# A hybrid decoder step on one core: prompt attention and paged decode rewritten as 16 steps in the order of the text

## The chip, the cores and the metric

One Trainium2 chip, of which the kernel uses one core. The metric is the device time of one execution in microseconds, given as the median of several runs. TensorE (PE in the profile, with PEld for its weight loads) does the matrix products and the transposes, VectorE (DVE) and ScalarE (ACT) the elementwise work and the copies out of PSUM, GpSimd (POOL) little, and SyncE (SP) issues the transfers.

## The reference, cut to what matters

One layer of a hybrid decoder, for a prompt of 1024 tokens and for 8 sample tokens (one each) that stand behind 4096 cached positions. The model width is 1024, all in float32.

```python
def hybrid_layer(x, pos, lw, gla_mix, mla_attend):
    x = x + 0.5 * swiglu(rms_norm(x, f1n), f1g, f1u, f1d)
    h = rms_norm(x, mix_n)
    q, k, v, g, a_low, c_q, c_kv, k_pe_raw = jnp.split(h @ w_in, offsets, axis=-1)
    o_gla, S = gla_mix(*gla_inputs(q, k, v, a_low, w_a_up, b_a))
    y_gla = gla_output(o_gla, g, g_norm)
    q_nope, q_pe, lat, k_pe = mla_project(c_q, c_kv, k_pe_raw, pos, q_norm, kv_norm, w_uq)
    y_mla = mla_attend(q_nope, q_pe, lat, k_pe, w_uk, w_uv)
    x = x + jnp.concatenate([y_gla, y_mla], axis=-1) @ w_out
    x = x + 0.5 * swiglu(rms_norm(x, f2n), f2g, f2u, f2d)
    return x, lat, k_pe, S
```

The change lies in `mla_attend`. For the prompt, each of 4 heads makes keys (`lat @ w_uk`) and values (`lat @ w_uv`) from a latent of 128 numbers per token, rotates 64 of the query's numbers by position, and takes a causal softmax over 1024 positions. For the samples the latents of the past are gathered by a page table (32 pages of 128 positions for each of 8 samples), the queries are taken into the latent's space (`q_lat = q_nope @ w_uk`), and the softmax runs over 4097 positions.

## The kernel before, in words

Products that must keep float32 accuracy are made of three (`mm3`, L87): each operand is split into a high part in the fast format and a rest (`split`, L83: ScalarE copies the high part, VectorE subtracts it), and high times high, high times low and low times high are summed in one PSUM bank. The stages follow each other: first feed-forward (0 to 717 us), input projection (to 850), the linear attention (GLA, to some 1021), prompt attention with paged decode (to 1314), output projection (to 1411), second feed-forward (to 2099).

A generator `pages` copies cache pages into gathered buffers in DRAM (`kvd`, `ped`); `beside(n)` (L199) takes its next n copies, which SyncE issues at that place. It is called in each block of `seven` (L295) in the first feed-forward, in the input projection (L761), and once for all that is left ahead of `levels(0, ..)` (L1051).

The paged decode has 16 units, `dec_unit(g, u)` (L1191): 2 groups of 4 samples by 8 stretches of 512 positions. A unit loads four tiles `kvt` and four `pet` (six buffers each), turns them on TensorE (16 transposes of `kvt`, 8 of `pet`, four to a bank, which ScalarE copies to `latT` and VectorE to `peT`), makes the scores (`dsc`), takes VectorE's maximum (`stat`) and ScalarE's exponential (`dpp`), turns that (VectorE copies it to `dpT`), multiplies it with `kvt` and keeps the result in `oc`. All its PSUM tiles rotate through the two banks of `psD`. `dec_combine(g)` joins a group's units and the new token.

Two units are run beside the end of GLA. Then the prompt's heads follow: for each pair of heads the rotary queries (`qpr`, `qs`) and all eight value tiles, for each head both key tiles, and for each block m of 256 queries `scores(m)` (L1366), the turns and products of the block before (`outputs`, L1414), and one decode unit. `scores` makes the queries, the products for two tiles of 128 queries (`sc`, three banks), the row maximum, the exponentials into one tile `pp` of 1024 columns, and scales it by the reciprocal of the sum. `outputs` turns `pp` in groups of four into `pT_h` and `pT_l` (three buffers each) and multiplies them with the values into `po` (one bank), whose split is `ym_h`, `ym_l`. Queries, keys, values and the turns of `pp` share the two banks `psA_`.

The order of the work on each engine is set when the kernel is built: a scheduler that keeps the tiles' dependencies orders instructions by their priority, which falls in the order of the text, and it may move one ahead of another. At run time each engine takes its instructions in that order.

Of the kernel before, what the change touches and what calls it, by code (L numbers as in the profile page):

```python
# [67 lines left out]
def hybrid_step(ctx: ExitStack, tc: tile.TileContext, I, O, C):  # L68
# [226 lines left out]
    def seven(A, todo):  # L295
# [3 lines left out]
        for i in (1, 6, 2, 7, 5, 3, 4):  # L299
# [18 lines left out]
            beside()  # L318
# [438 lines left out]
    def win_tile(src, evict, wt=None, blocks=BLKS3):  # L757
        if wt is None:
            wt = win_weights(src)
        h, l, n = wt  # L760
        beside(2)  # L761
# [74 lines left out]
    def rope(pool_, tag, dst, src, n, s):  # L836

        L = s.stop - s.start
        W = 512 if tag == "pp" else BL
        w = pool_.tile([P, 2 * W], F32, name="ropew", tag=tag, bufs=3 if tag == "pp" else 1)  # L840
# [101 lines left out]
    def levels(qr, st):  # L942
# [6 lines left out]
        for li, sz in enumerate((64, 32, 16, 8, 4, 2, 1)):  # L949
            qt = qts[nq[0] % 2]  # L950
            nq[0] += 1
            E = gk.tile([P, 2, 256], F32, name="E", tag="E")
# [98 lines left out]
    beside(len(units) * 16)  # L1051
# [99 lines left out]

    early_raw = []
    for srcs in ([qnd[:, 0]], [qnd[:, 1]], [latd], [kpd, kpd]):
        raw = rawp.tile([P, SEQ], F32, name="raw", tag="raw")
        w = P // len(srcs)
        for i, src in enumerate(srcs):
            ld.dma_start(raw[i * w:(i + 1) * w], src)
# [4 lines left out]
    psD_cm, psd = pool("psD", 2, space=PSUM, side="right")  # L1162

    def dbank(name="pd"):
        return psd.tile([P, 512], F32, name=name, tag="pd")
# [6 lines left out]
    oT = ep.tile([P, NS, 32], F32, name="oT", bufs=1)  # L1172
    uv = ep.tile([P, 4, P], F32, name="uv", bufs=1)
    ld.dma_start(uv, w_uv)
    grp = {}

    def fetch(g, u):

        kvt = [ep.tile([P, J, P], F32, name="kvt", tag="kvt", bufs=6) for _ in range(4)]
        pet = [ep.tile([P, J, 64], F32, name="pet", tag="pet", bufs=6) for _ in range(4)]  # L1180
# [3 lines left out]
        return kvt, pet  # L1184
# [6 lines left out]
    def dec_unit(g, u):  # L1191

        if u == 0:
            grp[g] = (ep.tile([P, 3, NU + 1], F32, name="stat", tag="stat"), ep.tile([P, NU + 1, P], F32, name="oc", tag="oc", bufs=1))
        oc = grp[g][1]
        kvt, pet = fetch(g, u)
        sc = dbank("dsc")
        lt, pe = [], []
        for b2 in range(2):
            p = dbank()  # L1200
            for q in range(4):
                PE.transpose(p[:, q * P:(q + 1) * P],
                             pet[2 * b2 + q // 2][:, 2 * (q % 2):2 * (q % 2) + 2, :].rearrange("p j c -> p (j c)"), ident)
            peT = ep.tile([P, 512], F32, name="peT", tag="peT")
            V.tensor_copy(peT, p)
            pe += [peT[:, :256], peT[:, 256:]]
        for bi in range(4):
            p = dbank()
            for q in range(4):
                PE.transpose(p[:, q * P:(q + 1) * P], kvt[bi][:, 2 * (q % 2) + q // 2, :], ident)  # L1210
            lt.append(ep.tile([P, 512], F32, name="latT", tag="latT", bufs=4))
            S.activation(lt[bi], p, AF.Copy)
        rows = [slice(32 * bi, 32 * bi + 32) for bi in range(4)]
        for bi in range(4):
            PE.matmul(sc[rows[bi], :], qlp[:, 4 * g + bi], lt[bi], start=True, stop=False)  # L1215
        for par in range(2):
            for bi in range(4):
                PE.matmul(sc[rows[bi], par * 256:par * 256 + 256], qpp[par][:, 4 * g + bi], pe[bi], start=False, stop=par == 1)  # L1218
        pp = ep.tile([P, 512], F32, name="dpp", tag="dpp")
        softmax(g, u, sc, 512, pp)  # L1220
        pT = ep.tile([P, J, P], F32, name="dpT", tag="dpT")
        p = dbank()
        for q in range(4):
            PE.transpose(p[:, q * P:(q + 1) * P], pp[:, q * P:(q + 1) * P], ident)
        V.tensor_copy(pT.rearrange("p j q -> p (j q)"), p)
        po = dbank()
# [3 lines left out]
        V.tensor_copy(oc[:, u], po[:, :P])  # L1230

    def dec_combine(g):
        stat, oc = grp[g]

        p = dbank()
        for bi in range(4):
            b = 4 * g + bi
            PE.matmul(p[32 * bi:32 * bi + 32, :NS], qlp[:, b], lat_s, start=True, stop=False)
            PE.matmul(p[32 * bi:32 * bi + 32, :NS], qpp[0][:64, b], kp_s, start=False, stop=True)
        sn = ep.tile([P, NS], F32, name="sn", tag="sn")  # L1240
        V.tensor_add(sn, p[:, :NS], newmask[:, g * NS:(g + 1) * NS])
        pn = ep.tile([P, NS], F32, name="pn", tag="pn")
        softmax(g, NU, sn, NS, pn)
        p = dbank()
        PE.transpose(p[:NS, :P], pn, ident)
        pnT = ep.tile([NS, P], F32, name="pnT", tag="pnT", bufs=1)
        V.tensor_copy(pnT, p[:NS, :P])
        p = dbank()
# [3 lines left out]
        cm = ep.tile([P, 4], F32, name="cm", tag="cm")  # L1252
        V.tensor_reduce(cm[:, 0:1], stat[:, 0, :], AX.X, OP.min)
        S.activation(stat[:, 2, :], stat[:, 0, :], AF.Exp, bias=cm[:, 0:1], scale=-1.0)
        V.tensor_mul(stat[:, 1, :], stat[:, 1, :], stat[:, 2, :])
        V.tensor_reduce(cm[:, 2:3], stat[:, 1, :], AX.X, OP.add)
        V.reciprocal(cm[:, 3:4], cm[:, 2:3])
        om = ep.tile([P, P], F32, name="om", tag="om", bufs=1)
        V.tensor_scalar_mul(om, oc[:, 0], stat[:, 2, 0:1])
        for u in range(1, NU + 1):  # L1260
            V.scalar_tensor_tensor(om, oc[:, u], stat[:, 2, u:u + 1], om, op0=OP.mult, op1=OP.add)
        V.tensor_scalar_mul(om, om, cm[:, 3:4])
        p = dbank()
# [428 lines left out]
```

## Time and profile before

| what | value |
|---|---|
| median of 3 runs | 2098.72 us (2098.38 to 2100.55) |
| the profiled execution | 2100.9 us |
| its span | 2099.1 us |
| its mean granted clock of TensorE | 0.989 |
| TensorE, VectorE, ScalarE busy | 2031.5, 1471.5, 838.0 us |

The span goes from the first to the last recorded instruction, and 1.8 us of the execution's time lie around it. The profiled execution is 2.2 us over the median of the runs. In the rows below, "PEclk" is the granted clock as a share of full speed, "idle before" is the time in which the engine did nothing ahead of an instruction, and "<-" names what ended it.

### The profile page before, as it was taken

To read this page: it belongs to the slowest core of one execution; us is meant where nothing else is said; L and a number is where in the kernel's file an instruction comes from. 1 tells how busy PE (TensorE), PEld (TensorE's weight loads), DVE (VectorE), ACT (ScalarE), POOL (GpSimd) and SP (SyncE) were. 2 spreads that over 40 slices of the span, in tenths; PEclk is the share of its full clock that TensorE was granted. 3 is DMA by queue.
4 is the path that set the end of the run, shared out by engine and by line. 5 is a ranking of instruction groups with operands and counts; after the bars stand their busy time and mean duration, and the time that the engine had idled before them with its cause. 6 is when DMAs were issued, how large, how long until landed. Compare 5 with 4: busy or idle time off the path is not lost.

```text
span 2099.1 us, 42793 instructions
## 1 busy us (share of the span) xinstructions
PE 2031.5 (97%) x16379; PEld 1915.6 (91%) x16379; DVE 1471.5 (70%) x2902; ACT 838.0 (40%) x1563; POOL 64.1 (3%) x95
## 2 busy tenths in 40 slices
PE   9999999999999999889899999999999999999997
PEld 8999999999999988888667777799999999999997
DVE  7876676675777865766565766488777778766775
ACT  7432322233344530436554644244323323333534
POOL 0000000000000000311000000000000000000000
PEclk9999999999999999999999999999999999999999
DMA  6444445467565623012443342744323233574352
GB/s 215 130 144 141 127 126 152 131 203 265 159 187 152 166 75 99 11 42 81 129 129 96 115 128 60 221 136 122 91 92 121 87 88 122 159 260 146 110 158 92
DMA packets 235837, 276.46 MB, mean 132 GB/s; under 512 B 27216, under 2 KB 186128, under 8 KB 235632
## 3 DMA queue, kind: packets, MB, share of 16 engines
q1 hardware_dynamic: 235632, 273.72, 42.7%
q8 instruction: 129, 2.11, 0.4%
q14 instruction: 76, 0.62, 0.1%
HBM read 214.34 MB, written 84.47 MB: 142 GB/s over the span
## 4 chain that ended last, share of the span: by engine, by line
PE 80%; DVE 8%; DMA 3%; ACT 3%; issue 2%; SPq 1%; POOL 1%; POOLq 0%; DVEq 0%; ACTq 0%
PE pp L93 34%; PE pp L448 20%; PE pw L93 6%; PE pr L93 4%; PE po L93 1%; PE pd L1210 1%; PE pw L1076 1%; PE dsc L1215 1%; DVE al L85 1%; PE pg L973 1%; PE ps L93 1%; PE dsc L1218 1%; PE ps L1423 1%; PE pd L1229 1%; DMA kvt<-kvd 1%
## 5 line engine op out<-in xcount | busy, mean ns | idle before, releaser
L93 PE MATMUL pp<-bh,ah 128*128 128x260 f32 (+1 forms) x2432 | 688.3, 283 | 9.7 <-DVE u L310 6.8
L93 PE MATMUL pp<-bl,ah 128*128 128x260 f32 (+1 forms) x2432 | 687.1, 283 | 1.8 <-DVE bl L85 1.8
L93 PE MATMUL pp<-bh,al 128*128 128x260 f32 (+1 forms) x2432 | 687.0, 283 | 0.6 <-DVE al L85 0.6
L93 PEld LDWEIGHTS pp<-bh,ah 128*128 128x128 f32 x2432 | 460.7, 189 | 12.1 <-DVE u L310 7.8
L93 PEld LDWEIGHTS pp<-bh,al 128*128 128x128 f32 x2432 | 462.1, 190 | 1.7 <-DVE al L85 1.7
L93 PEld LDWEIGHTS pp<-bl,ah 128*128 128x128 f32 x2432 | 459.8, 189 | 2.4 <-DVE bl L85 2.4
L448 PE MATMUL pp<-th,dl 128*128 128x256 f32 x1232 | 248.6, 283 | 1.2 <-DVE dl L85 1.2
L448 PE MATMUL pp<-tl,dh 128*128 128x256 f32 x1232 | 248.9, 283 | 0.1
L448 PE MATMUL pp<-th,dh 128*128 128x256 f32 (+1 forms) x1232 | 248.9, 283 | 0.0
L84 ACT ACTIVATE ah<-raw 128x512 fp32r<-128x512 f32 x208 | 128.8, 627 | 236.5 <-PE pp L93 219.0
L448 PEld LDWEIGHTS pp<-tl,dh 128*128 128x128 f32 x1232 | 190.0, 189 | 2.4 <-DVE tl L85 2.4
L448 PEld LDWEIGHTS pp<-th,dl 128*128 128x128 f32 x1232 | 189.9, 188 | 1.4 <-DVE dl L85 1.4
L448 PEld LDWEIGHTS pp<-th,dh 128*128 128x128 f32 x1232 | 190.8, 189 | 0.1
L84 ACT ACTIVATE dh<-a 128x1024 fp32r<-128x1024 f32 (+1 forms) x84 | 83.0, 988 | 253.9 <-PE pp L448 226.5
L85 DVE TENSOR_TENSOR al<-raw,ah 128x512 fp32r<-128x512 f32 x208 | 142.3, 688 | 48.7 <-ACT ah L84 47.2
L85 DVE TENSOR_TENSOR dl<-a,dh 128x1024 fp32r<-128x1024 f32 (+1 forms) x84 | 95.3, 1134 | 114.5 <-ACT dh L84 108.1
L84 ACT ACTIVATE ah<-sl 128x512 fp32r<-128x512 f32 x132 | 82.9, 630 | 201.0 <-PE pp L93 154.0
L93 PE MATMUL pw<-xh,wh 128*128 128x260 f32 (+4 forms) x320 | 101.1, 316 | 0.0
L93 PE MATMUL pw<-xh,wl 128*128 128x260 f32 (+4 forms) x320 | 100.5, 314 | 0.0
L93 PE MATMUL pw<-xl,wh 128*128 128x260 f32 (+4 forms) x320 | 100.1, 313 | 0.0
L85 DVE TENSOR_TENSOR tl<-traw,th 128x1032 fp32r<-128x1032 f32 (+1 forms) x84 | 95.6, 1138 | 3.8 <-ACT th L84 3.6
L85 DVE TENSOR_TENSOR al<-sl,ah 128x512 fp32r<-128x512 f32 x132 | 90.5, 688 | 10.9 <-ACT ah L84 8.1
(426 smaller groups left out, 3571.1 us busy)
## 6 DMA issues: line engine op xcount, KB each, us to landing
traw<-td SPq DMA_DIRECT2D x70, 516.0 KB
raw<-in_ffn_w_gate_dram SPq DMA_DIRECT2D x52, 512.0 KB
raw<-in_ffn_w_up_dram SPq DMA_DIRECT2D x52, 512.0 KB
a<-in_ffn_w_down_dram SPq DMA_DIRECT2D x40, 512.0 KB
kvd<-in_cache_kv_dram SPq DMA_DIRECT2D x256, 64.0 KB
kvt<-kvd SPq DMA_DIRECT2D x64, 256.0 KB
td<-q SPq DMA_DIRECT2D x22, 520.0 KB
td<-q SPq DMA_DIRECT2D x22, 512.0 KB
```

Source lines behind the costliest of these rows:

```text
L84: S.activation(out_h, src, AF.Copy)
L85: eng.tensor_sub(out_l, src, out_h)
L93: PE.matmul(ps, w_, x_, start=i == 0, stop=i == n - 1)
L448: PE.matmul(bank[c][m], w_[:, kk, ms], x_[:, kk, c * N[0]:c * N[0] + N[c]], start=first and j == 0 and (c == 1 or m % 2 == 0), stop=last a ...
L973: PE.matmul(p[:, t, c], kt[:, t, c * P:(c + 1) * P], qt[:, t, :, c * 64:(c + 1) * 64], start=True, stop=True)
L1076: PE.matmul(p[:n, :256], x_[:, k], w_[:, k % 4, :], start=i == 0, stop=i == 3 * KD - 1)
L1210: PE.transpose(p[:, q * P:(q + 1) * P], kvt[bi][:, 2 * (q % 2) + q // 2, :], ident)
L1215: PE.matmul(sc[rows[bi], :], qlp[:, 4 * g + bi], lt[bi], start=True, stop=False)
L1218: PE.matmul(sc[rows[bi], par * 256:par * 256 + 256], qpp[par][:, 4 * g + bi], pe[bi], start=False, stop=par == 1)
L1229: PE.matmul(po[rows[bi], :P], pT[:, (j % 2) * 2 + j // 2, rows[bi]], kvt[bi][:, j], start=j == 0, stop=j == J - 1)
L1423: PE.transpose(p[:, jj, qi * P:(qi + 1) * P], prs[qi][:, (j + jj) * P:(j + jj + 1) * P], ident)
```

## The change

- `beside` is called in three of seven blocks of the first feed-forward, with 4 in place of 2 in the projection, with 4 in each level of GLA, and no longer for all that is left ahead of the levels.
- A transfer slot of the pool `raw` is loaded early with the first head's weights and the mask (`first_w`). The rotary key is loaded later.
- The decode unit is cut into `turn(0)` to `turn(5)`, `dec_scores`, `dec_softmax`, `dec_turn`, `dec_values`. `kvt` has 11 buffers, `pet` 8, and a unit is fetched two units ahead. The unit has one bank of its own (`sc_`) for its scores, the turned probabilities and its values.
- Three banks (`psA_`) serve the decode's turns, the turns of `pp`, the queries, keys, values and rotary tiles. The prompt's scores keep three banks, `po` one.
- `pp` is a tile of 512 columns for each part (six buffers); `pT_h` and `pT_l` have two buffers in place of three.
- Keys, values and rotary queries of the next head are made in the steps before it; rotary queries in two parts (`loads=True` makes the product, the swapped copy and the product with the cosine; the second call adds the sine's part and splits).
- 16 steps (h, m) are written out. From `first` on, all instructions of TensorE, ScalarE and VectorE are chained, so that each engine takes them in the order of the text.

The core of the diff:

```diff
-            beside()
+            if i in (6, 7, 3):
+                beside()
...
-    beside(len(units) * 16)
     levels(0, sts[0])
...
-        kvt = [ep.tile([P, J, P], F32, name="kvt", tag="kvt", bufs=6) for _ in range(4)]
-        pet = [ep.tile([P, J, 64], F32, name="pet", tag="pet", bufs=6) for _ in range(4)]
+        kvt = [ep.tile([P, J, P], F32, name="kvt", tag="kvt", bufs=11) for _ in range(4)]
+        pet = [ep.tile([P, J, 64], F32, name="pet", tag="pet", bufs=8) for _ in range(4)]
...
-            for m in range(4):
-                prs = scores(m)
-                if pend:
-                    outputs(*pend)
-                pend = (m, prs, h, hh, v_h, v_l)
-                decode(1)
...
+    psD_cm, unit_bank = pool("psU", 1, space=PSUM, side="right")
+    ps_cm, ps = pool("psA_", 3, space=PSUM)
+    psd = ps
...
+    def rotary(t, b, loads=False):
+        s, qs = slice(512 * b, 512 * b + 512), qs_
+        if loads:
+            p, wt = bank(), W["r", t]
+            mm3(p, [(wt[0][:, k], wt[1][:, k], qn_h[:, k, s], qn_l[:, k, s]) for k in range(2)])
+            w = rawp.tile([P, 1024], F32, name="ropew", tag="raw")
+            ld.dma_start(w[:, :512], C["cos"][:, s])
+            ld.dma_start(w[:, 512:], C["sin"][:, s])
...
+            qpr = ap_.tile([P, 512], F32, name="qpr", tag="qpr", bufs=1)
+            V.tensor_mul(qpr, p, w[:, :512])
+            Rot[t, b] = w, sw, qpr
+            return
...
+    steps = [(h, m) for h in range(4) for m in range(4)]
+    old = None
+    for i, (h, m) in enumerate(steps):
+        unit, after, third = [units[j] if j < len(units) else None for j in range(i, i + 3)]
...
+        if third:
+            fetch(*third)
+        s0 = scores(h, m, 0)
+        d(dec_scores)
+        maximum(*s0)
+        pr0 = exps(*s0, 0)
+        d(dec_softmax)
+        t(0)
+        s1 = scores(h, m, 1)
+        maximum(*s1)
+        factor(*s0)
+        if old:
+            old.turn(0)
+            old.part(0)
+            old.turn(1)
+            old.part(1)
+        pr1 = exps(*s1, 1)
+        tick()
+        t(4)
+        d(dec_turn)
...
+        t(1)
+        if old:
+            old.turn(2)
+            old.product(0)
+            old.part(2)
+        scale(pr0, s0[1])
+        factor(*s1)
...
+        t(5)
+        if old:
+            old.turn(3)
+            old.product(1)
+            old.part(3)
...
+        d(dec_values)
+        if new:
+            queries(*new)
+        scale(pr1, s1[1])
+        t(2)
...
+        t(3)
+        if old:
+            old.product(3)
+            old.out()
...
+    for ins in list(traced[first:]):
+        if ins.engine in (mybir.EngineType.PE, mybir.EngineType.Activation, mybir.EngineType.DVE):
+            if ins.engine in last:
+                tc.add_manual_dep(ins, last[ins.engine].name, mybir.DependencyInfo(
+                    mybir.DependencyClass.NoSync, mybir.DependencyReason.DATA), reason="in the order of the text")
+            last[ins.engine] = ins
```

How this moves instructions, at three places. First TensorE in a step, from the queries of a block to the unit's scores. Before, in the second half of the attention's first pair of heads (`dsc` are the unit's scores, `pd` the turns):

```order
L93 MATMUL ps<-qn_h,uql 128x256
L1210 MATMUL pd<-ident,kvt 128x128 x4
L1387 MATMUL sc<-k_h,q_h 128x384
L1210 MATMUL pd<-ident,kvt 128x128 x4
L1388 MATMUL sc<-k_l,q_h 128x384
L1210 MATMUL pd<-ident,kvt 128x128 x4
L1389 MATMUL sc<-k_h,q_l 128x384
L1210 MATMUL pd<-ident,kvt 128x128 x4
L1390 MATMUL sc<-kp_h,qs_15184 128x384
L1215 MATMUL dsc<-latT,qlp 32x512 x4
L1218 MATMUL dsc<-peT,qpp_11185 32x256 x4
```

After, in the first steps (`pt` are the turns, `sc__15509` the unit's bank):

```order
L93 MATMUL ps<-qn_h,uql 128x256
L1204 MATMUL pt<-ident,kvt 128x128 x8
L1452 MATMUL sc<-k_h,q_h 128x384
L1453 MATMUL sc<-k_l,q_h 128x384
L1454 MATMUL sc<-k_h,q_l 128x384
L1455 MATMUL sc<-kp_h,qs_15198 128x384
L1456 MATMUL sc<-kp_l,qs_15198 128x384
L1458 LDWEIGHTS identb
L1458 MATMUL sc<-causalb,identb 128x128
L1223 MATMUL sc__15509<-latT,qlp 32x512 x4
L1228 MATMUL sc__15509<-peT,qpp_10217 32x256 x4
```

Before, a unit's scores follow its last turns by one product of the prompt; now the eight last turns are followed by all scores of a query tile, and then by the unit's.

Second, VectorE between the first decode unit's probabilities and the second's, after the change (`sc__15029` is the bank of the first unit, `sc__15127` of the second, `ropew` the rotary table):

```order
L1241 COPY dpT<-sc__15029 128x512
L85 TENSOR_TENSOR uql<-first_w,uqh 128x256
L1252 COPY oc<-sc__15029 128x128
L85 TENSOR_TENSOR qn_l<-raw,qn_h 128x1024 x2
L1209 COPY peT<-pt 128x512 x2
L1214 TENSOR_REDUCE stat<-sc__15127 128x1
L1409 TENSOR_TENSOR qpr<-ps,ropew 128x512
L1241 COPY dpT<-sc__15127 128x512
```

Before, the splits of `qn` stood ahead of the first unit's `dpT`, and the second unit's `dpT` ahead of all work with the rotary table.

Third, SyncE there, after the change (`ped_3_88` and `kvd_3_72` are the pages of the fourth unit, `raw<-kpd` is the rotary key):

```order
L1194 DMA pet<-ped_3_88 128x256 x2
L1193 DMA kvt<-kvd_3_72 128x512
L1194 DMA pet<-ped_3_88 128x256 x2
L1402 DMA ropew<-const_cos_dram 128x512
L1403 DMA ropew<-const_sin_dram 128x512
L1539 DMA raw<-kpd 64x1024 x2
```

The rotary table stands behind the fourth unit's loads, which take the buffers of the second unit's `pet` and so come behind its turns. Before, both rotary tables (L842, L843) stood ahead of all loads of the third and fourth unit.

In the first feed-forward and the projection SyncE's order has the same page copies ahead of the same weight loads to within two of them, and TensorE's order is the same.

## Rows read from the trace of the kernel before

**Rows 1.** The page: busy time, share of the span and instructions of each engine.

```profile
PE 2031.5 (97%) x16379; PEld 1915.6 (91%) x16379; DVE 1471.5 (70%) x2902; ACT 838.0 (40%) x1563; POOL 64.1 (3%) x95
```

**Rows 2.** Stretches: window, us, busy PE, PEld, DVE, ACT, POOL, PEclk, DMA share, GB/s.

```profile
1021.00:1074.00 53.00, 43.68 (x317) 29.60 (x318) 34.14 (x73) 32.80 (x80) 2.68 (x3) 0.90 0.39 121
1074.00:1191.00 117.00, 113.75 (x1016) 86.07 (x1016) 73.84 (x184) 59.71 (x144) 0.00 (x0) 1.00 0.36 111
```

**Rows 3.** Groups of TensorE by shape, 1073.6 to 1311.4 us: busy us, mean ns.

```profile
L1210 PE MATMUL pd<-ident,kvt 128*128 128x128 f32 x208 | 31.1, 277 | 2.2 <-DMA kvt<-kvd 1.8
L1423 PE MATMUL ps<-ident,pp 128*128 128x128 f32 x160 | 26.7, 290 | 2.6 <-DVE pp L1408 1.7 <-DVE pT_l L85 0.6 <-DVE mx L1399 0.2
L93 PE MATMUL po<-pT_h,v_h 128*128 128x256 f32 x80 | 25.6, 320 | 1.1 <-ACT pT_h L84 0.7
```

**Rows 4.** Timeline of TensorE in a step: start us, us, engine, line, work, count.

```profile
1139.75 1.08 PE L1229 MATMUL pd<-kvt,dpT 128*32 128x128 f32 x32
...
1142.96 0.66 PE L1210 MATMUL pd<-ident,kvt 128*128 128x128 f32 x4
1143.37 0.48 PE L1389 MATMUL sc<-k_h,q_l 128*128 128x512 f32 x1
...
1146.15 1.43 PE L1215 MATMUL dsc<-latT,qlp 128*32 128x512 f32 x7
...
1148.81 0.38 PE L1389 MATMUL sc<-k_h,q_l 128*128 128x256 f32 x1
1149.03 0.28 PE L1390 MATMUL sc<-kp_h,qs 128*128 128x256 f32 x1
1149.15 0.28 PE L1391 MATMUL sc<-kp_l,qs 128*128 128x256 f32 x1
...
1149.62 0.39 PE L1388 MATMUL sc<-k_l,q_h 128*128 128x512 f32 x1
1149.86 0.40 PE L1389 MATMUL sc<-k_h,q_l 128*128 128x512 f32 x1
```

**Rows 5.** Waits from 1021 to 1314 us: us in total, times, longest.

```profile
PEld dsc L1215 <- ACT latT L1212: 9.8, 25, 1.4
...
PEld pd L1210 <- ACT latT L1212: 5.7, 14, 1.0
...
PEld sc L1387 <- ACT q_h L84: 4.9, 10, 0.8
...
PEld pd L1210 <- DVE peT L1205: 4.8, 11, 1.8
```

**Rows 6.** Timeline of all engines ahead of the first prompt scores, idle time in brackets.

```profile
1040.31 0.69 DVE L1225 COPY dpT<-pd 128x512 f32<-128x512 f32 x1
1040.91 1.22 DVE L85 TENSOR_TENSOR kp_l<-raw,kp_h 128x1024 fp32r<-128x1024 f32 x1
1041.05 1.94 PE L1229 MATMUL pd<-kvt,dpT 128*32 128x128 f32 x32 [2.86 <-DVE dpT L1225]
...
1044.08 0.33 SPq L1301 DMA_DIRECT2D causal<-const_causal_dram  x1
...
1045.45 0.47 SPq L842 DMA_DIRECT2D ropew<-const_cos_dram  x1
...
1045.66 0.42 DVE L85 TENSOR_TENSOR uv_l<-uv,uv_h 128x256 fp32r<-128x256 f32 x1
...
1047.54 0.23 DVE L1305 CAST causalb<-causal 128x128 bf16<-128x128 f32 x1 [1.46 <-DMA causal<-const_causal_dram]
...
1054.75 0.69 DVE L848 TENSOR_TENSOR sw<-sw,ropew 128x512 f32<-128x512 f32 x1 [0.83 <-ACT sw L847]
...
1073.79 0.39 PE L1387 MATMUL sc<-k_h,q_h 128*128 128x256 f32 x1
```

**Rows 7.** Timeline of TensorE at the end of the attention, idle time in brackets.

```profile
1302.44 1.49 PE L1423 MATMUL ps<-ident,pp 128*128 128x128 f32 x6 [1.70 <-DVE pp L1408]
...
1313.76 0.47 PE L93 MATMUL pr<-yg_h,wh 128*128 128x512 f32 x1 [2.83 <-DVE ym_l L85]
```

More of the change, by code (lines that the diff above doesn't have):

```diff
@@ L760, in win_tile @@
         h, l, n = wt
-        beside(2)
+        beside(4)
         for s in blocks:
@@ L1189, in softmax, with dec_scores @@
         S.activation(pout[:, :n], sc[:, :n], AF.Exp, bias=stat[:, 0, u:u + 1], accum_out=stat[:, 1, u:u + 1])
-    def dec_unit(g, u):
+    def dec_scores(g, u):
         if u == 0:
[L1194 to L1206, printed above, removed]
-        for bi in range(4):
[L1208 to L1215, printed above, removed]
@@ L1216, in dec_unit @@
+            grp[g] = [ep.tile([P, 3, NU + 1], F32, name="stat", tag="stat"), None]
+        sc = dbank("sc")
+        live[g, u] = [sc]
+        for bi in range(4):
+            PE.matmul(sc[rows[bi], :], qlp[:, 4 * g + bi], turned.pop((g, u, bi)), start=True, stop=False)
+        pe = [turned.pop((g, u, 4 + b2)) for b2 in range(2)]
         for par in range(2):
             for bi in range(4):
-                PE.matmul(sc[rows[bi], par * 256:par * 256 + 256], qpp[par][:, 4 * g + bi], pe[bi], start=False, stop=par == 1)
@@ L1219, in dec_unit @@
[L1219 to L1222, printed above, removed]
[L1223 to L1226 removed]
+                o = 256 * (bi % 2)
+                PE.matmul(sc[rows[bi], par * 256:par * 256 + 256], qpp[par][:, 4 * g + bi], pe[bi // 2][:, o:o + 256],
+                          start=False, stop=par == 1)
@@ new lines, in values, with keys, queries @@
+    def values(t, j):
+        js, (uv_h, uv_l) = slice(j * P, (j + 1) * P), UV[t]
+        p = bank()[:, :256]
+        for i, (l_, r_) in enumerate(((lat_h, uv_h), (lat_l, uv_h), (lat_h, uv_l))):
+            PE.matmul(p, l_[:, js], r_, start=i == 0, stop=i == 2)
+        split(v_h[:, j], v_l[:, j], p)
+    def keys(h, b):
+        s = slice(b * 512, b * 512 + 512)
+        p = bank()
+        mm3(p, [(*UK[h], lat_h[:, s], lat_l[:, s])])
+        split(k_h[:, s], k_l[:, s], p)
+    def queries(h, m):
+        p = bank()[:, :256]
+        wt, s = W[h], QB[m]
+        mm3(p, [(wt[0][:, k], wt[1][:, k], qn_h[:, k, s], qn_l[:, k, s]) for k in range(2)])
+        Qm[h, m] = [ap_.tile([P, 256], F32R, name=f"q_{z}", tag=f"q_{z}") for z in "hl"]
+        split(*Qm[h, m], p)
@@ new lines, in hybrid_step @@
+    load_uqr(0)
+    split(qn_h[:, 0], qn_l[:, 0], early_raw[0])
+    split(qn_h[:, 1], qn_l[:, 1], early_raw[1])
+    rotary(0, 0, loads=True)
+    load_uk(0)
+    split(lat_h, lat_l, early_raw[2])
+    load_uq(0)
+    keys(0, 0)
+    queries(0, 0)
+    load_uv(0)
+    turn(*units[0], 0)
+    kraw_ = rawp.tile([P, SEQ], F32, name="raw", tag="raw")
+    for i in range(2):
+        ld.dma_start(kraw_[64 * i:64 * i + 64], kpd)
+    rotary(0, 0)
+    turn(*units[0], 4)
+    split(kp_h, kp_l, kraw_)
@@ L1439, in hybrid_step @@
+    uv = rawp.tile([P, 4, P], F32, name="uvr", tag="raw")
+    ld.dma_start(uv, w_uv)
+    old.turn(0)
+    old.turn(1)
+    old.part(0)
+    old.part(1)
+    tick(20)
+    old.turn(2)
+    old.product(0)
     for h in range(4):
-        p = dbank()
+        p = bank()
         PE.matmul(p[:, :NS], uv[:, h], oT[:, :, h], start=True, stop=True)
         split(ym_h[:, h, SEQ:], ym_l[:, h, SEQ:], p[:, :NS])
+    old.part(2)
+    old.turn(3)
+    old.product(1)
+    old.part(3)
+    old.product(2)
@@ L1443, in hybrid_step @@
+    old.product(3)
+    old.out()
+    last = {}
+    for ins in list(traced[first:]):
[4 more added lines that the diff above has]
+            last[ins.engine] = ins
     close(a_cm)
```

401 lines of the change are left out of this document (257 added, 144 removed).

## The prediction

> **What bounds the kernel now.** I read the page first, then the stretches around the change, then the timeline and the waits inside them. The page says that TensorE is the bound: it is busy 97% of the span, VectorE 70%, ScalarE 40% [rows 1]. In the attention stages the share alone says little. From 1074 to 1191 us TensorE is busy 114 of 117 us at full clock, VectorE 74 and ScalarE 60 [rows 2]. But a busy TensorE is not a TensorE at its pace: the mean of a 256-column product is 320 ns [rows 3], while two that follow each other without a wait start 0.12 us apart [rows 4]. So I price the work by the distance of such starts and call all the rest of the stretch its excess.
>
> The paces [rows 4]: 0.12 us for a 256-column matmul (1149.03 to 1149.15), 0.24 for 512 columns, less in long series (I use 0.118 and 0.231; 384 columns are put between them at 0.175), 0.41 for four turns (transposes; 0.109 each), 2.66 for a decode unit's scores (this unit's, with small waits in it; I use 2.5), 1.08 for its values, of which the last 0.07 overlap what follows. A decode unit with 28 turns is then 3.05 + 2.5 + 1.0, about 6.57 us.
>
> Between the first prompt scores, 1073.79 [rows 6], and the end of the last prompt product, 1313.76 less the 2.83 of idle time, 1310.9 [rows 7], TensorE has: 13 units (208 turns of `kvt`, 16 a unit [rows 3]), 85.4 us; scores of 24, 8 and 16 pieces of 512, 384 and 256 columns with five products each (by the code's widths and its 32 query tiles), 5 x 8.83 = 44.2, with 2.3 for the mask; 240 products with the values (three groups like the one of 80 [rows 3]), 28.3; 160 turns of probabilities [rows 3], 17.4; queries, keys, values and one pair of rotary tiles, 20.4; the decode's small ends and the rest of a unit, 4. That is 202 us of 237.1. **The excess is 35 us**, and it is what the change can win in this stretch. Nearly 6.5 of it is the end: a wait of 1.70 us for the scaled probabilities, slow matmuls behind it (six turns take 1.49 us at 1302.44) and more small waits; the 2.83 us in which the output projection waits for `ym_l` come on top [rows 7]. About 7 lie, by the same count, at the three changes of head. The remaining 21 or so are the steps' waits: TensorE waits for the unit's turned rows (`latT`, 9.8 us in 25 waits), for a bank whose copy isn't done (5.7 and 4.8), for the queries' split (4.9) [rows 5]. These numbers include the stage ahead of the first scores and partly lie under running matmuls.
>
> **The change part by part.** *Page copies* (`beside` in `seven`, `project`, `levels`): SyncE issues the same page copies ahead of the same loads to within two of them, and TensorE's order in the first feed-forward is the same. I cost it at zero, with 2 us to either side for the few loads that move in the linear attention.
>
> *Before the first scores.* Up to unit 0's probabilities (`dpT`, 1040.31 [rows 6]) little moves. From there VectorE's order after the change holds, up to the first reduction of prompt scores, 18 operations on 512 columns at 0.69 us, 6 on 256 at 0.42, 5 small ones (1.3 together), and 4 splits on 1024 at 1.22 (0.69, 0.42 and 1.22 as `dpT`, `uv_l` and `kp_l` take [rows 6]): 12.4 + 2.5 + 1.3 + 4.9 = 21.1 us. TensorE has some 17 us of work in that time, so VectorE sets the pace. Without any wait the first reduction stands at 1061.4. In the same stretch of the kernel before VectorE had some 11 us of waits. The splits of `qn` and `lat` were earlier there, beside the linear attention, and six value tiles and a key tile that stood ahead of the first scores now come later. A new wait stands here: SyncE issues the rotary table only behind the `pet` loads of unit 3, which wait for unit 1's turns of `pet`, and VectorE's product with it stands ahead of unit 1's `dpT`. The nearest rows: a load issued at 1044.08 had VectorE waiting till 1047.54, 3.5 us after its issue, and the old rotary table, issued at 1045.45, was used 9.3 us later without a wait for it [rows 6]. So the wait costs VectorE between nothing and 7 us; I take 3, and 2 to 3 us for the rest. First reduction near 1067, first scores near 1066, bounds 1060 and 1072.
>
> *Work behind the first scores.* 202 us become 207.6: unit 2's scores and part of its work (+2.5), one key tile (+0.7) and six value tiles (+2.1) move behind.
>
> *The steps.* The turns for unit n+1 now stand a whole step ahead of its scores, and the two fetches ahead let the data land. The wait for `latT` goes, because the first prompt scores (1.3 to 4.5 us of TensorE) and eight turns lie between the last copy and its use. Queries have four to eight turns and other tiles between the split (0.38 + 0.42 us) and the scores. The unit's softmax (0.69 + 0.69 + 0.2 us) is covered by the second query tile's scores and the old step's turns. What is late next: `pT_h`/`pT_l` have two buffers in place of three, so the fourth group of turns is followed by a split that waits for the first products; the second tile's scores wait for a bank of three until the first tile's exponentials are out. Walking the text of one head with these durations I find 0.8 us of stall in step m=0, and 0.1, 0.2, 0.3 in the others: 5.6 us over four heads; 2.7 at the head changes, where `k_l` of the next head is ready less than half a microsecond ahead; 2 for the new rotary tiles, whose two halves let VectorE work between; 2 where a group is combined; 3 in the first step and in the last two, which have no unit to hide their softmax; 7.5 at the end, whose chain is as before; and 6 for what such a walk does not see (16 steps at 0.4, as a first matmul of another kind starts 0.1 late). Sum 29 us for 35. VectorE has about 8 to 12 us a step against TensorE's 11 to 16, so it stays under.
>
> *Sum.* 1066 + 207.6 + 29 = 1302.6 against 1310.9: 8.3 us less. What follows is untouched; `ym_l` is waited for as before. The profiled execution took 2100.9 us (span 2099.1), so 2092.6 by the profile, and as it lies 2.2 above the median of the three runs (2098.72), **2090.4, or 2090 us**. About 0.2%, 4.2 us, is what a measurement can tell from no change.
>
> **The rivals.** *More.* The fixed order takes nearly all steps' waits: only the end (6.5), the head changes (4) and 5 for the rest remain, excess 16, and the sum is 1290, 21 us less: 2077. For it speaks that TensorE alone bounds the steps; against it that each step still has three chains through VectorE and ScalarE.
>
> *No gain.* The accumulators aren't more than before: the decode's two banks and the prompt's two become one for the unit and three for all the rest, and about as many tiles pass through them. If the waits on a bank ([rows 5], 5.7 and 4.8) come from their number, they stay, and with them the steps' 21 us: excess 35, 1066 + 207.6 + 35 = 1308.6, 2.3 us less, 2096. [...]
>
> *Slower.* Fixed order on three engines: what stands first holds all behind it. VectorE stops at the rotary table, unit 1's `dpT` and all splits wait behind it, and TensorE behind them: with 7 us there the first scores come at 1072. In the steps one late split of probabilities stops the copies of the unit behind it; at 0.6 us a step more than in my walk (16 x 0.6 = 9.6) the excess is 39: 1072 + 207.6 + 39 = 1318.6, 7.7 more, 2106. It decides where start and excess together pass 1107.5 us (mine: 1095). [Rows 6] show such a stop: TensorE waited 2.86 us for `dpT`, which stood behind other work of VectorE, and the 32 products after it took 1.94 us in place of 1.08 [rows 4, 6], in a stage with a mean granted clock of 0.90 [rows 2]. [...]
>
> **How the numbers follow.** My forecast has 0.44, *more* 0.22, *no gain* 0.17, *slower* 0.17. Faster by over 0.2%: 0.44 + 0.22 = 0.66; within 0.2%: 0.17; slower: 0.17. The range takes the start's bounds and an excess from 17 to 40: 2074 (just past *more*) to 2104, short of the full price of *slower*.
>
> **What would show it.** In the changed profile: the first prompt scores at 1060 to 1072; the last prompt product ending near 1303; no wait of TensorE for `latT` worth 2 us in all; VectorE waiting for the rotary table by 1 to 5 us ahead of unit 1's `dpT`; feed-forward stages of the same length to 2 us. I am wrong if TensorE waits for `pT_h` or for a bank by over a microsecond in each step, if the first scores come after 1075, or if the difference lies outside the attention.

## The result, and the profile after

The change makes the kernel slower: 2110.65 us (median of 8 runs, 2105.40 to 2116.03) against 2098.60 (8 runs), a ratio of 1.0056, 95% interval 1.0044 to 1.0069. That is 12 us, outside the stated range (2074 to 2104) and on the other side. The profiled execution took 2109.42 us, 8.5 more than the one of before. TensorE is still the busiest engine: the same 16379 instructions, with 9 us less busy time in a longer span. Page of the changed kernel (compare [rows 1]), then its stretches (compare [rows 2]):

```profile
PE 2022.2 (96%) x16379; PEld 1910.7 (91%) x16379; DVE 1475.4 (70%) x2918; ACT 840.1 (40%) x1565; POOL 65.6 (3%) x95
```

```profile
1021.00:1074.00 53.00, 40.19 (x276) 25.39 (x279) 29.90 (x63) 28.65 (x71) 3.03 (x3) 0.88 0.49 153
1074.00:1191.00 117.00, 108.48 (x1037) 85.91 (x1030) 73.17 (x187) 57.76 (x143) 0.00 (x0) 0.96 0.36 111
```

TensorE is busy 5 us less in the steps' first half, and its granted clock, full before, is 0.96 on average. The output projection starts at 1322.4 us in place of 1313.8: the whole difference of the two profiles lies ahead of it. From 1021 us to that start TensorE is idle for 37.8 us, 20.6 before. Its timeline shows the stops (idle time and what ended it in brackets):

```profile
1062.50 1.11 PE L1204 MATMUL pt<-ident,pet 128*128 128x128 f32 x4 [3.42 <-ACT latT L1207]
...
1070.37 0.56 PE L1452 MATMUL sc<-k_h,q_h 128*128 128x256 f32 x1
...
1169.52 0.45 PE L1297 MATMUL pt<-ident,om 128*128 128x128 f32 x1 [4.95 <-DVE om L1294]
1169.90 1.94 PE L1251 MATMUL sc__16513<-kvt,dpT 128*32 128x128 f32 x32
...
1194.95 0.50 PE L93 MATMUL ps<-qn_h,uqh 128*128 128x512 f32 x1 [1.42 <-ACT latT L1207]
...
1302.62 0.50 PE L1452 MATMUL sc<-k_h,q_h 128*128 128x512 f32 x1 [2.31 <-ACT pp L1473]
...
1311.70 1.42 PE L1503 MATMUL ps<-ident,pp 128*128 128x128 f32 x11 [1.55 <-DVE pp L1488]
...
1322.36 0.40 PE L93 MATMUL pr<-yg_h,wh 128*128 128x512 f32 x1
```

The first scores start at 1070.37 (1073.79 in [rows 6]). Then come few stops, but long ones, each ended by another engine. Behind the longest two TensorE runs on slowly: the granted clock is 0.50 from 1062.5 to 1066.6 and from 1169.5 to 1173.2 us, and the 32 products behind the stop of 4.95 us take 1.94 us, 1.08 in [rows 4]. Behind the stops of 1.42 and 1.55 us it is 1.00. The projection no longer waits for `ym_l` ([rows 7], 2.83 us); the decode's last products do, 1.22 us at 1316.58.

The waits for `latT` answer to [rows 5]. The scores' wait for their data (9.8 us before) is nearly gone, but turns now wait for a bank that a late copy to `latT` must free. Before, these were waits of the weight loads (PEld), and the products themselves waited only 0.5 us for `latT`; now the products (PE) wait too:

```profile
PEld pt L1204 <- ACT latT L1207: 13.4, 11, 3.6
...
PE pt L1204 <- ACT latT L1207: 10.2, 6, 3.4
...
PE pt L1297 <- DVE om L1294: 5.4, 2, 4.9
...
PEld sc__16997 L1223 <- ACT latT L1207: 2.0, 1, 2.0
```

ScalarE and VectorE show why the copy is late. ScalarE, changed kernel, ahead of the first scores and in the step with the new rotary tiles:

```profile
1059.60 1.28 ACT L1417 ACTIVATE qs<-qpr 64x512 fp32r<-64x512 f32 x2 [1.44 <-DVE qpr L1414]
1060.90 1.06 ACT L84 ACTIVATE kp_h<-raw 128x1024 fp32r<-128x1024 f32 x1
1061.87 0.58 ACT L1207 ACTIVATE latT<-pt 128x512 f32<-128x512 f32 x1
...
1192.72 1.28 ACT L1417 ACTIVATE qs<-qpr 64x512 fp32r<-64x512 f32 x2 [3.68 <-DVE qpr L1414]
1194.03 0.38 ACT L84 ACTIVATE q_h<-ps 128x256 fp32r<-128x256 f32 x1
1194.31 0.59 ACT L1207 ACTIVATE latT<-pt 128x512 f32<-128x512 f32 x1
```

The copies to `qs` wait for VectorE's sum, and `latT`, whose turns end at 1058.7 and 1192.1 us, waits behind them (1061.87 and 1194.31). VectorE at the stop of 4.95 us, the chain that combines a group's eight units, with TensorE's turn of its result next in the text:

```profile
1165.99 3.06 DVE L1291 SCALAR_TENSOR_TENSOR om<-oc,stat,om 128x128 f32<-128x128 f32 x8
1169.09 0.29 DVE L1294 TENSOR_SCALAR om<-om,cm 128x128 f32<-128x128 f32 x1
```

The median holds a noise from outside the attention: in 20 profiles with the same order of TensorE up to there, the input projection starts between 713.6 and 722.6 us. So I also give, for each kernel, the time from the start of the last input projection product (at 1005 to 1016 us, beside the end of GLA) to that of the first output projection product, in two parts (A up to the first prompt scores, B from there), read from the first and last starts of `pw`, `sc` and `pr` in its trace. It comes from one profile of each kernel and is not free of noise either: below, 2 us of it change where two kernels have the same text. The profile of f3 is its longest run, 11 us over its median, and that of f4 is 6 us over.

| kernel | A | B | A + B | median us | ratio to before, 95% interval |
|---|---|---|---|---|---|
| before | 63.9 | 240.0 | 303.9 | 2098.60 | 1 |
| the change | 60.8 | 252.0 | 312.8 | 2110.65 | 1.0056 (1.0044 to 1.0069) |
| e1 free order | 46.3 | 234.9 | 281.2 | 2074.42 | 0.9894 (0.9877 to 0.9910) |
| e2 turn of `om` later | 60.4 | 247.5 | 307.9 | 2106.20 | 1.0038 (1.0024 to 1.0053) |
| e3 split of rotary later | 59.2 | 246.7 | 305.9 | 2099.45 | 1.0003 (0.9989 to 1.0017) |
| e4 page copies alone | 63.2 | 239.8 | 303.0 | 2099.80 | 1.0008 (0.9997 to 1.0019) |
| f1 fixed in the steps only | 47.0 | 258.1 | 305.1 | 2099.81 | 0.9998 (0.9985 to 1.0011) |
| f2 TensorE fixed | 52.0 | 235.8 | 287.8 | 2086.77 | 0.9929 (0.9913 to 0.9946) |
| f3 ScalarE fixed | 50.7 | 245.7 | 296.4 | 2085.85 | 0.9924 (0.9907 to 0.9940) |
| f4 VectorE fixed | 53.5 | 251.9 | 305.4 | 2100.65 | 0.9998 (0.9986 to 1.0009) |
| m1 VectorE free | 58.3 | 243.7 | 302.0 | 2097.89 | 0.9981 (0.9965 to 0.9997) |
| m4 no chain of `om` | 60.5 | 242.6 | 303.1 | 2105.76 | 1.0018 (1.0007 to 1.0030) |
| h1 text mended, fixed | 58.8 | 252.0 | 310.8 | 2108.86 | 1.0040 (1.0026 to 1.0054) |
| n1 the same, old end | 58.0 | 247.1 | 305.1 | 2102.05 | 0.9992 (0.9979 to 1.0005) |
| h2 text mended, free | 47.9 | 236.5 | 284.4 | 2081.04 | 0.9904 (0.9887 to 0.9920) |
| n2 free, e3's split | 48.0 | 234.3 | 282.3 | 2081.02 | 0.9888 (0.9858 to 0.9919) |
| g3 free, one unit ahead | 48.0 | 235.3 | 283.3 | 2080.68 | 0.9907 (0.9890 to 0.9923) |
| g4 free, banks apart | 46.0 | 247.0 | 293.0 | 2092.54 | 0.9955 (0.9938 to 0.9972) |
| m2 free, weights late | 46.3 | 235.5 | 281.8 | 2078.76 | 0.9904 (0.9876 to 0.9933) |
| m3 free, priority, one bank | 45.7 | 237.1 | 282.8 | 2086.01 | 0.9920 (0.9901 to 0.9939) |

Each ratio is to runs of before on the same chip, whose medians go from 2098.4 to 2102.8 us. So ratios, not medians, compare kernels of different rows: a step of 0.001 is 2.1 us.

### The profile page after: what moved, and what is told of

Its sections match the earlier page's. It is cut to its first block, busy times and chain, and to the rows that moved or that the text cites. A ratio compares the mean times of both kernels' runs of the same rounds, so it can differ in the third digit from the quotient of the medians.

```text
span 2107.7 us, 42815 instructions
## 1 busy us (share of the span) xinstructions
PE 2022.2 (96%) x16379; PEld 1910.7 (91%) x16379; DVE 1475.4 (70%) x2918; ACT 840.1 (40%) x1565; POOL 65.6 (3%) x95
## 4 chain that ended last, share of the span: by engine, by line
PE 80%; DVE 9%; ACT 4%; DMA 3%; issue 2%; POOL 1%; SPq 1%; POOLq 0%; DVEq 0%; ACTq 0%
PE pp L93 38%; PE pp L449 18%; PE pw L93 5%; PE pr L93 4%; DMA raw<-in_ffn_w_gate_dram 2%; PE pt L1204 1%; PE ps L93 1%; PE pw L1077 1%; PE po L1520 1%; DMA xraw<-x2d 1%; DVE qt L971 1%; PE pg L975 1%; PE ps L1503 1%; DVE pT_l L85 1%; DVE al L85 0%
## 5 line engine op out<-in xcount | busy, mean ns | idle before, releaser
L85 DVE TENSOR_TENSOR al<-sl,ah 128x512 fp32r<-128x512 f32 x132 | 90.1, 685 | 12.1 <-ACT ah L84 9.5
```

Source lines behind the costliest of these rows:

```text
L85: eng.tensor_sub(out_l, src, out_h)
```

## The experiments

**The fixed order, undone as a whole.** Theory: the loss is in stops behind instructions that the text puts too early.

```diff
-            if ins.engine in last:
+            if False and ins.engine in last:
```

> The change without the chain that fixes the order of TensorE, ScalarE and VectorE; the scheduler is free again. Theory: the loss comes from stops behind instructions that the text puts too early (the turn of om, the split of the rotary queries), so a free order gives back part of it, 2098 to 2105 us. Rival: the loss comes from the shared banks and the work itself, whatever the order, so 2108 to 2114 us.

Measured 2074.42 us: 36 less than the change, and 24 less than before (34 and 22 by the ratios). The theory had it too small, and the rival was wrong. All else of the change together is a gain; fixing the three engines to the order of the text turns it into a loss. The free order is an order too, set by the scheduler when the kernel is built: what loses is the order of this text. SyncE, which no fixed order holds, moves with it (the first rotary table is issued at 1032.75 us in place of 1049.22), and that was not tried apart; the wait for this table is 1.50 us in the change. From 1021 us to the output projection TensorE is idle for 11.3 us here, 37.8 in the change; that is some 26 of the 32 us in A + B. TensorE with the free order, around the same turn of `om`, then the stretches:

```profile
1148.38 0.27 PE L1297 MATMUL pt<-ident,om 128*128 128x128 f32 x1
1148.59 1.08 PE L1251 MATMUL sc__16513<-kvt,dpT 128*32 128x128 f32 x32
```

```profile
1021.00:1074.00 53.00, 47.90 (x400) 30.80 (x399) 36.03 (x79) 34.17 (x84) 2.06 (x2) 1.00 0.53 164
1074.00:1191.00 117.00, 115.52 (x1098) 91.50 (x1097) 83.11 (x208) 66.27 (x159) 0.00 (x0) 1.00 0.38 122
```

At this place there is no wait and no slow product, and the clock is full in both stretches. The scheduler had VectorE do the chain earlier, in single links between other work (its last two at 1140.27 and 1140.65):

```profile
1140.27 0.34 DVE L1291 SCALAR_TENSOR_TENSOR om<-oc,stat,om 128x128 f32<-128x128 f32 x1
...
1140.65 0.35 DVE L1291 SCALAR_TENSOR_TENSOR om<-oc,stat,om 128x128 f32<-128x128 f32 x1
...
1141.06 0.27 DVE L1294 TENSOR_SCALAR om<-om,cm 128x128 f32<-128x128 f32 x1
```

Where they lie shows in the distance between the value products (`dec_values`) of one decode unit and the next (units counted from 0), in us, from the timelines:

| from unit to unit | change | free order |
|---|---|---|
| 1 to 2 (ahead of the first step's end) | 24.5 | 17.7 |
| 2 to 3 (first step) | 10.9 | 8.8 |
| 3 to 4, 4 to 5, 5 to 6, 6 to 7 (a head's steps) | 16.2, 17.0, 15.7, 12.1 | 16.1, 16.1, 14.7, 12.1 |
| 7 to 8 (first group combined) | 19.4 | 13.9 |
| 8 to 9, 9 to 10 (rotary tiles of the next heads) | 19.8, 22.3 | 15.6, 18.5 |
| 15 to the end of the last product | 37.7 | 32.9 |

The ordinary steps differ by at most a microsecond, the first by 2.1. The five distances 1 to 2, 7 to 8, 8 to 9, 9 to 10 and the end make 25.1 us.

**One engine fixed, or one free.**

```diff
-        if ins.engine in (PE, Activation, DVE):
+        if ins.engine in (PE,):
```

(Written without `mybir.EngineType.`; `Activation`, `DVE`, or `PE, Activation` for the others.)

> Only TensorE's order is fixed. Theory (the queues of ScalarE and VectorE hold the turns): TensorE's own order costs only the stops at the turn of om, 2078 to 2086 us. Rival (TensorE stands still because of its own order): 2100 to 2112.

> Only ScalarE's order is fixed. Theory: ScalarE's waits for the rotary sums with the copies of the turns behind them are the larger part, 2090 to 2105 us. Rival: 2073 to 2080, ScalarE has time to spare and its order costs nothing.

> Only VectorE's order is fixed. Theory: VectorE's chain of om and its place behind the rotary table cost some 5 us, 2077 to 2085. Rival: 2095 to 2110, VectorE's order is the cause and ScalarE's only follows it.

> TensorE and ScalarE fixed, VectorE free. Theory (VectorE's order is the cause): 2084 to 2092 us, near the runs with one of the two fixed. Rival (any two fixed orders lock each other): 2098 to 2110.

By the ratios TensorE's order alone costs 7 us over the free one, ScalarE's 6, VectorE's 22; by A + B 7, 15 and 24 (ScalarE's 15 from its longest run). For TensorE the time was nearly the theory's (2086.77 for at most 2086), but what TensorE waits for is `latT` (2.84 us at 1062.04), and there is no stop over 0.9 us at the turn of `om`. For ScalarE the time lies between the theory and the rival, and for VectorE it is the rival's. But VectorE is not the only cause: with it free and the two others fixed, 21 of the 32 us of A + B stay (2097.89, at the rival's lower edge). The other two pairs were not run. The parts don't add, since one stop can come from any of several orders: TensorE waits for the turn of `om` 4.07 us with VectorE alone fixed, 3.44 with ScalarE alone, and 4.39 with VectorE alone free.

**The order fixed from the first step on.** `first` is taken anew where `steps` is made.

> The order of the three engines is fixed from the first of the 16 steps on; the work ahead of them is left to the scheduler. Theory: about half of the 36 us between the fixed and the free order lie ahead of the first scores (1070 against 1052), so 2089 to 2095 us. Rival 1: all of it is in the steps, what is won ahead is lost again behind the first scores, 2106 to 2112. Rival 2: all of it ahead, 2074 to 2078.

The time fell to 2099.81 us, but by A + B only by 7.7: A is as short as in the free order, and B becomes longer than in the change (258.1 against 252.0), since more work lies behind the first scores. The time lies between the theory and rival 1. So 24 of the 32 us of A + B come with the order of the steps alone.

**The suspected places, one by one.** First the turn of `om` behind the next instructions of TensorE:

```diff
         V.tensor_scalar_mul(om, om, cm[:, 3:4])
+        done.add(g)
         yield
...
-        if unit and unit[1] == 0:
-            tick(20)
+        while slack and unit and unit[1] == 0 and 0 not in done:
+            tick()
         d(dec_values)
```

> The first group's turn of om is put behind the unit's values and the next queries, no longer directly behind its chain on VectorE. Theory: TensorE's stop of 4.92 us at 1164.57 and the slow matmuls behind it go, 5 to 8 us less than the change. Rival: VectorE's chain of some 3.4 us itself delays the step, the stop moves to another wait, less than 2 us gained.

4 us less by the ratios (their intervals overlap), 4.9 by A + B, a little under the theory, but not at the place that it names. From unit 7 to 8 it takes 14.0 us in place of 19.4, from 8 to 9 22.2 in place of 19.8, from 9 to 10 23.5 in place of 22.3: 3.6 of the 5.4 us come back in the next steps, as the rival has it. TensorE's stop for `om` is still 2.59 us, at its new place. The other 3 us lie ahead of unit 2 (22.3 in place of 24.5) and at the end (36.9). The first of these is not the edit's doing, as it touches nothing there. In both kernels TensorE stops for `latT` twice ahead of the first scores (3.42 and 1.94 us in the change, 3.53 and 1.94 here), but then the granted clock was 0.50 from 1069.6 to 1075.4 us in the change, and 1.00 from 1067.2 to 1070.4 here. The scores of unit 2, of the change and then of e2:

```profile
1071.85 1.94 PE L1223 MATMUL sc__15374<-latT,qlp 128*32 128x512 f32 x8
1073.56 1.93 PE L1228 MATMUL sc__15374<-peT,qpp 128*32 128x256 f32 x16
```

```profile
1068.41 1.15 PE L1223 MATMUL sc__15374<-latT,qlp 128*32 128x512 f32 x8
1069.29 1.12 PE L1228 MATMUL sc__15374<-peT,qpp 128*32 128x256 f32 x16
```

So what the edit itself brought is some 2 to 3 us.

Then the split of the rotary queries, apart from their sum:

```diff
         V.tensor_add(qpr, qpr, sw)
+        Rot[t, b] = qpr
+
+    def rot_split(t, b):
...
         for hh in range(2):
...
+            if h == 1:
+                rot_split(1, 0)
             keys(h + 1, 0)
```

> The split of the rotary queries (ScalarE's two copies, VectorE's two differences) is put some turns later than the sum that it needs, so that ScalarE no longer waits 3.7 and 1.8 us there with the copies of the turns behind it. Theory: of the stops ahead of the first scores and in the step of the new rotary tiles (together some 12 us of waits for latT) 5 to 8 us go. Rival: the four swap copies of ScalarE (2.4 us each time) and not the wait hold the turns, less than 2 us gained.

11 us less by the ratios, 6.9 by A + B: by the ratio to before (1.0003) this one edit undoes the loss, by A + B 2 us of it stay. From unit 1 to 2 it takes 19.0 us in place of 24.5 (some 2 of these 5.5 are the clock, an estimate: from the start of the first scores to the turns behind unit 2's scores it is 2.8 us here, 1067.36 to 1070.13, and 5.1 in the change, 1070.37 to 1075.42, at a granted clock of 0.50), from 9 to 10 18.5 in place of 22.3. ScalarE's copies to `qs` wait 0.35 us once, 1.44, 3.68 and 1.81 in the change. The swap copies are as before, so the wait in the queue, not their work, held the turns.

Last the chain itself, without its eight multiply-adds:

> The change with the eight multiply-adds of each group's chain of om left out, so that the decode's result holds the first unit alone. Theory: of the 36 us some 9 go (the stop of 4.9 us with the slow matmuls behind it, and 2 to 3 at the end), 2100 to 2104. Rival: they are 6 us of VectorE's work that others hide, 2107 or more.

A + B falls by 9.7 us, near the 9 expected, and by the ratios it is 8; the time itself, 2105.76, lies between the theory and the rival. Some 2 of the 9.7 us lie from unit 1 to 2 (22.8 in place of 24.5), where no chain stands. From 7 to 8 it takes 16.2 us in place of 19.4, and TensorE still waits 1.85 us for the turn of `om`. The end takes 34.8 us in place of 37.7, and the stop of 2.31 us for a bank of the scores is gone. In the change the chain's links stand there ahead of a row maximum, on which ScalarE's exponential waits (VectorE, then ScalarE, of the change):

```profile
1299.38 1.12 DVE L1291 SCALAR_TENSOR_TENSOR om<-oc,stat,om 128x128 f32<-128x128 f32 x3
1300.42 1.15 DVE L1464 TENSOR_REDUCE mx<-sc 128x1 f32<-128x512 f32 x2
```

```profile
1301.79 0.69 ACT L1473 ACTIVATE pp<-sc,mx 128x512 f32<-128x512 f32 x1 [4.85 <-DVE mx L1466]
```

**The suspected places mended together.** e2 and e3, the turns ahead of the first step moved forward, the rest of the second rotary tile put into that step, one bank for the last products, and in the steps without a unit:

```diff
+        if old and not unit:
+            for j in range(2):
+                old.turn(j)
+                old.part(j)
         s1 = scores(h, m, 1)
...
-        tick()
+        tick(1 if unit else 3)
```

> All three engines fixed in the order of the text, but the text is mended at the places where a queue stops: the turn of om later, the split of the rotary queries apart from their sum, the last turns of unit 2 ahead of the second rotary tile, whose rest goes into the first step, the old turns ahead of the second tile's scores in steps without a unit, and one bank for the last four products. Theory (the fixed order costs only where the text puts a waiting instruction ahead of ready ones): 2080 to 2091 us. Rival (a fixed order costs everywhere, by small waits in each step): 2093 to 2102, the two mends measured so far and little more.

Neither: 2108.86 us. The mended places are shorter (1 to 2 takes 21.0 us, 7 to 8 14.0, 9 to 10 18.5), but 8 to 9 takes 22.2 us in place of 19.8, as in e2, and the end 44.8 in place of 37.7. There pieces of the chain now stand ahead of the last queries' split. VectorE, then TensorE, of this kernel:

```profile
1287.03 1.11 DVE L1291 SCALAR_TENSOR_TENSOR om<-oc,stat,om 128x128 f32<-128x128 f32 x3
1288.05 0.42 DVE L85 TENSOR_TENSOR q_l<-ps,q_h 128x256 fp32r<-128x256 f32 x1
```

```profile
1288.52 0.79 PE L1460 MATMUL sc<-k_h,q_l 128*128 128x512 f32 x1 [3.15 <-DVE q_l L85]
```

I had made a new stop while taking others away. With this part taken back:

> The mended text in the fixed order, without the mend of the steps that have no unit (old turns and three pieces of the chain of om at one place). Theory: the end goes back from 44.8 to some 37 us behind the last unit, so 2095 to 2102 us. Rival: the end was not the cause, 2106 to 2110.

2102.05 us, at the upper edge of the theory, the end at 39.9 us. Even so A + B stays 24 us over the free order. From 8 to 9 this text takes 22.3 us, the free order 15.6, with a stop of 2.59 us for the turn of `om`; its end is 7.0 us longer than the free order's, with stops of 2.33 us for a bank of the scores, 1.52 for `pp` and 1.57 for `ym_l`. So it is shown that the three orders together make the loss, and at single places how. Mending these places left most of it, and whether a text of this kind can be written without the loss stays open.

The mended text with the scheduler free, and e3's split alone:

> The mended text with the scheduler free. Theory: the scheduler moves waiting instructions back by itself, so that the mends bring it little, 2068 to 2076 us. Rival: the mended text helps it as much as the fixed order, 2060 or less.

> The free order with the split of the rotary queries apart from their sum. Theory: the scheduler had moved the split already, 2072 to 2080 us. Rival: a gain as in the fixed order, 2063 to 2069.

2081.04 and 2081.02 us, above what both theories and both rivals have, and no gain over e1 (ratios 0.9904 and 0.9888 against 0.9894, A + B 284.4 and 282.3 against 281.2). The mends bring the scheduler's order nothing: in e1 the copies to `qs` wait at most 0.62 us, and there is no stop over 1 us ahead of the end.

**What the free order's gain rests on.** All with the free order: `kvt` in 8 buffers and units fetched one step ahead; the decode's turns in one bank of their own and two for the rest; `first_w` loaded behind the early units; the old priority of the probabilities' split with one bank for the last products.

> The free order, with kvt in 8 buffers in place of 11 and each unit fetched one step ahead in place of two. Theory: the turns then wait for their data at the start of steps, 2078 to 2090 us. Rival: one unit ahead is enough, 2072 to 2077.

> The free order, with the three shared banks cut into one for the decode's turns and two for all else. Theory: the sharing is part of the gain, since six turns of a unit in one bank wait for their copies each time (0.6 to 0.7 us): 2080 to 2095 us. Rival: sharing is worth nothing, 2072 to 2077.

> The free order with the loads of the first head's weights and the mask issued behind the two early units, where the kernel before had them. Theory: the weights then arrive late and the first scores come 3 to 8 us later, 2077 to 2083 us. Rival: they arrive in time, 2073 to 2077.

> The free order with the raised priority of the probabilities' split that the kernel before had, and one bank for the last four products. Theory: the end shortens by 1 to 3 us, 2071 to 2074. Rival: no change or a loss, 2074 to 2080.

Sharing the three banks is worth 12 us by A + B (13 by the ratios): theory met. The second unit ahead is worth 2, the early slot under 1 by A + B. The times of g3 and m2 lie in their theories' ranges, but not for the theories' reasons: in g3 TensorE waits 0.4 us in all for a unit's data behind 1050 us, in m2 A is 46.3 us as in e1, and the intervals of both ratios overlap e1's. m3 gained nothing and falls out of both expectations; its profile starts the attention 8 us later than e1's, A + B is 1.6 us longer, and its interval overlaps e1's too.

**Page copies alone** (on the kernel before):

> The kernel before with only the changed places of the page copies. Prediction and theory: within 2 us of before. Rival: the copies shift loads in the first feed-forward, 3 us or more to either side.

The interval takes in no change, 0.9997 to 1.0019, and A + B is 0.9 us shorter: no effect is seen, as predicted.

e1, the change without its last loop, has the lowest median and the shortest A + B of the study: 0.9894 of the kernel before. The intervals of h2, n2, g3, m2 and m3 overlap its own.

## Why the prediction was wrong

- *Page copies at zero*: right as far as seen (e4). The sign of feed-forward stages equal to 2 us was missed, with 716.6 and 719.3 us to the input projection, within the spread of the 20 profiles.
- *First scores near 1066, bounds 1060 to 1072*: 1070.37, within them. The new wait at the rotary table was the smaller part: VectorE stood idle 1.50 us ahead of that product (1052.60). The profile names ScalarE's `dpp` for it, but the last piece of the table landed at 1052.51. The larger one was ScalarE's stop at `qs` (TensorE 3.42 us), which I didn't have; without it (e3) A is only 1.6 us shorter, so the lateness of 4.4 us is not all explained. With the free order the scores come at 1051.88: my 21 us of VectorE's work as a floor held only for the text's order, since the scheduler began the scores with the parts that need no rotary tile (the rotary ones start at 1054.78).
- *Work behind the first scores, 207.6 us*: its terms add to 207.3; I keep 207.6 as the base. One price in it was too high. I put 2.5 us for a unit's scores from a row with waits in it; with all turns done ahead, 12 of the 14 units behind the first scores take 1.86 us in the change, as here:

```profile
1176.87 1.06 PE L1223 MATMUL sc__16738<-latT,qlp 128*32 128x512 f32 x8
1177.75 1.05 PE L1228 MATMUL sc__16738<-peT,qpp 128*32 128x256 f32 x16
1178.73 0.66 PE L1204 MATMUL pt<-ident,kvt 128*128 128x128 f32 x4
```

  Over 14 units that is 9 us which I held for fixed work and which the change does take away; the excess below hides them.
- *The steps' excess, 29 us*: **this is the step that failed.** From 1070.37 to 1322.53, where the last product ends, it is 252.2 - 207.6 = 44.6 us. I walked TensorE's text and asked whether each thing it needs is ready; I did not walk the queues of ScalarE and VectorE where an unusual item stands in them. So the ordinary steps came out about right (within a microsecond of the free order), partly by luck. By the same paces the ten distances from 2 to 7 and 10 to 15 hold some 10 us of excess with 2.5 us for the scores and 16 with 1.86, an estimate; I had given them some 9. The unusual places came out too small: 2 us for combining a group (5.5 measured against the free order), 2 for the rotary tiles (8.0), and the end, where I gave 7.5 "as before" and the chain of `om` came on top, with the wait for a bank of the scores behind it (4.8 over the free order). Together these are 14 of the 15.6 us; that they add up so is a reading of the intervals, not an experiment.
- *The wait for `latT` goes*: half right. As a wait for data it went; as a wait for the bank behind a blocked copy it came back, larger (13.4 us of PEld, 5.7 in [rows 5]).
- *`ym_l` is waited for as before*: wrong, to the good side. The last product ended 20 us late, but without these 2.83 us the output projection starts only 17 us late (1322.36 against 1302.6 + 2.83). The median is 20 us late all the same, since the profiled run of before lay 2.2 us over its median and that of the change 1.2 under.
- *The range*: its own bounds (1060 with 17, 1072 with 40) give 2072 to 2107 us, wider than the stated one; the result lies outside both.
- The rival that ended slower had the right mechanism (one late item holds all behind it in a fixed queue, as `latT`, whose turns were done at 1058.7 us, ran at 1061.87 only behind `qs`, which had waited 1.44) at 0.17, with its point of decision, start plus excess over 1107.5 us; it was 1115.0. I priced it at 0.6 us in each step, while most of it sits in five places.
- *No gain, as the banks are no more*: the number alone doesn't decide. In the free order, sharing the same number of banks gave 12 us (g4).
- *More*, 2077 us: it had the fixed order take the waits. A time near it came without that order (2074), so the number is met by chance.

## What to carry to other kernels

A hand-written order must be walked on every queue it fixes, and above all at the items that come once in a while (a combine, a table, an end): the regular steps were within a microsecond of the scheduler's order here, and five irregular places held 25 us. Try a new structure with and without the fixed order before judging it: the same code gained 24 us or lost 12. A fix in a fixed order can make a stop elsewhere, so look at the whole trace after each.

## What the runs showed of the hardware that was not expected

- The first feed-forward isn't steady. With TensorE's order the same there, the input projection started between 713.6 us (e1) and 722.6 (g4) in the 20 profiles. The page's costliest group, of the change and then of e1:

```profile
L93 PE MATMUL pp<-bh,ah 128*128 128x260 f32 (+1 forms) x2432 | 687.5, 283 | 12.9 <-DVE u L310 10.4
```

```profile
L93 PE MATMUL pp<-bh,ah 128*128 128x260 f32 (+1 forms) x2432 | 687.3, 283 | 7.5 <-DVE u L310 6.3
```

  5.4 us of the two profiles' difference are idle time in the feed-forward stages, 4.1 of them behind VectorE (L310), and the two kernels have the same text there. Differences of a few microseconds are better read from the stretch that was changed than from the total.
- The stop of 4.95 us cost more than its length: behind it TensorE's granted clock was 0.50 from 1169.5 to 1173.2 us, where it was 1.00 from 1150.0 to 1164.5. Products of 256 columns then started 0.21 us apart (0.12 in [rows 4]). By the starts from 1169.90 to 1174.59 against those paces that is about 2 us more, an estimate. The price is not the same each time: behind nearly the same two stops ahead of the first scores (3.42 and 1.94 us in the change, 3.53 and 1.94 in e2) the granted clock was 0.50 until 1075.4 us in the change and 1.00 from 1067.2 in e2.
